# Two activation groups transposed per visit in the second feed-forward, and a ScalarE copy of the query projections ahead of their norm

## The chip, the cores and the metric

The kernel runs on one core of one Trainium2 chip. The metric is the device time of one execution in microseconds; before the change it is 2654.88 us, the median of three runs (2654.12 to 2655.74). The engines are named as the profile names them: PE is TensorE's matmul (PEld its weight load), ACT is ScalarE, DVE is VectorE, POOL is GpSimd, SP is SyncE.

## What is computed

One layer of a diffusion backbone over 256 latent tokens and 256 context tokens of width 2048, all in float32: a half-step SwiGLU feed-forward, a mixing sub-layer, and a second half-step SwiGLU on the latent tokens alone. The mixing sub-layer projects the tokens to the queries of 8 heads, keys and values of 2 heads, and the three inputs of a long convolution; a gate from one of the three is multiplied in at the end. The two places that the change touches are these:

```python
def q_heads(p_q, q_norm):
    B, L = p_q.shape[:2]
    return rms_norm(p_q.reshape(B, L, N_Q_HEADS, HEAD_DIM), q_norm)

def swiglu(h, w_up, w_down):
    gate, up = jnp.split(h @ w_up, 2, axis=-1)
    return (jax.nn.silu(gate) * up) @ w_down
```

Each head's 128 query values are divided by the root of their mean square, get a gain, are rotated (rope) and go into a softmax attention over 512 keys. The second feed-forward has 5632 hidden columns.

## The kernel before, in words

**Number format.** Every float32 operand of a large product is split into a high part (the float32 value rounded by an ACT cast) and a low part (the remainder, a DVE subtraction), and a product is three matmuls: high by high, high by low, low by high. For the weights `weight` does this (L207 to L229): a DMA of 512 KB into `raw` (four buffers), the cast L221 into `whi` (three buffers), the subtraction L225 into `wlo` (three buffers). For activations `split_to` does it (L201 cast, L202 subtraction).

**Buffers.** Most activation tiles come from one pool of 58 buffers of 2 KB per partition, tag `u` (function `U`). PSUM has two tags of four banks each: `pa` for the accumulations over the model width, `pb` for transposes, scores and the rest. The order of the instructions on each engine is worked out by a scheduler when the program is built: it starts from program order, and lets work that is ready go ahead of work that waits. So PE's order in the attention mixes several parts of the program.

**The queries.** Two groups of four heads (loop `qb`, L1068). For each group `proj_steps` (L822 to L834) accumulates two `pa` banks, one for each half of 128 tokens, over eight weight pieces (matmuls L831 to L833, 12 for a piece). The first group's projection is issued in steps among the long convolution's transforms (L232 to L234 at that place). Then `fill` issues the first half of the gate's first projection (`proj_pair`, matmuls L239, L240, L242, two more `pa` banks). `head_norm` (L865) takes one `pa` bank: Square on ACT (L869) out of PSUM, a sum over each head on DVE (L871), `rstd_from` (L262 to L271, with a Sqrt on ACT at L263), and a DVE multiply out of PSUM (L874) into a `u` tile. `gain_rope` (L877) asks for another `u` tile and applies gain and rotation in ten DVE operations (L882 to L899; its first result is L895). Four PE transposes (L1078) and a split follow, and `attend` runs scores, softmax (L1045 to L1051), transposes (L1058) and products for the two halves. The second query group's projection is the next user of `pa` after the gate's first one. `head_norm` is also called with two heads for the keys, four times.

**After the attention.** The rest of the gate (L240), the group norms (L1094 to L1102), and the output projection (`out_unit`, with `tok_mm`, L1118 to L1120), then the norm of the second feed-forward.

**The second feed-forward.** The up stage has 22 groups (`UPG`) of 256 hidden columns. A group has two `pa` banks (128 tokens each) and eight weight pieces of 12 matmuls (L1118 to L1120). At its end ACT makes Silu of the gate half (L1311), DVE multiplies the up half (L1312), and the result `at` holds 256 tokens by 256 columns with tokens on the partitions. The down stage needs it the other way round, so `turn_act` transposes it on PE into one `pb` bank (four transposes of 128x128, L1275) and splits that into two tiles (L201, L202). It is called for the group before, after the third weight piece of the current group (`kp == 2`); for the last group it is called in the down stage, at its third weight piece (`fq == 2`). The first 14 of the 44 split tiles have a pool of their own (`act`), the others are `u` tiles. The down stage has four column blocks of 22 weight pieces, again 12 matmuls for a piece.

Of the kernel before, what the change touches and what calls it, by code (L numbers as in the profile page):

```python
# [18 lines left out]
P = 128  # L19
D = 2048  # L20
KT = D // P
L = 256
# [33 lines left out]
def hybrid_layer_kernel(ctx: ExitStack, tc: tile.TileContext, a):  # L56
    nc = tc.nc
    V, S, G, PE = nc.vector, nc.scalar, nc.gpsimd, nc.tensor
    serial = [0]

    def T(pool, shape, tag, dt=F32, bufs=None):
        serial[0] += 1
        kw = {} if bufs is None else {"bufs": bufs}
        return pool.tile(list(shape), dt, tag=tag, name=f"{tag}_{serial[0]}", **kw)
# [6 lines left out]
    def U(shape, dt=F32):  # L71
        return T(up, shape, "u", dt, 58)

    def tmp(shape):
        return T(up, shape, "sq", bufs=2)

    def tmp2(shape):
        return T(up, shape, "sg", bufs=3)

    def PA(shape=(P, 512)):  # L80
        return T(pp, shape, "pa")

    def PB(shape=(P, 512)):
        return T(pp, shape, "pb")

    ident = T(const, (P, P), "ident")
# [91 lines left out]
    def ada_col(d):  # L178

        bank = ada_bank.pop(d)  # L180
        rows = tmp2((P, 2 * P))
        copied = S.copy(rows, bank[:, 0 : 2 * P])
        for j in range(2):
            last = PE.transpose(bank[:, (2 + j) * P : (3 + j) * P], rows[:, j * P : (j + 1) * P], ident)
        col = cols[d % 2]
        turned = bank[:, 2 * P : 4 * P].rearrange("p (j g c) -> p j c g", g=4, c=32)
        V.tensor_reduce(col, turned[:, :, 0:2, :], axis=AX.X, op=ALU.add)
        V.scalar_tensor_tensor(first_mod[:, 1, d, :], col[:, 0, :], bada1[:, d : d + 1],
                               gn[:, 0, d : d + 1].broadcast_to((P, 2)), op0=ALU.add, op1=ALU.mult)
        V.tensor_scalar(first_mod[:, 0, d, :], col[:, 1, :], bada[:, d : d + 1], None, op0=ALU.add)  # L190
        return copied, last, bank
# [8 lines left out]
    def split_to(src, hi, lo):  # L200
        S.copy(hi, src)  # L201
        V.tensor_sub(lo, src, hi.bitcast(F32))  # L202
        return hi, lo
# [55 lines left out]
    def rstd_from(ss, n, shape, pool_tile, y, root=None):  # L259

        m, e = pool_tile(shape), pool_tile(shape)
        mean = V.tensor_scalar(m, ss, 1.0 / n, EPS, op0=ALU.mult, op1=ALU.add)  # L262
        rooted = S.activation(y, m, AF.Sqrt)  # L263
        roots.append(rooted)
        if root:
            then(root(mean, rooted), V.reciprocal, y, y)
        else:
            V.reciprocal(y, y)
        V.tensor_mul(e, y, y)
        V.scalar_tensor_tensor(e, e, -0.5, m, op0=ALU.mult, op1=ALU.mult)  # L270
        return V.scalar_tensor_tensor(y, e, 1.5, y, op0=ALU.add, op1=ALU.mult)  # L271
# [277 lines left out]
    for i in range(2):  # L549
        for q in range(KT // 2):  # L550
            t = U((P, 2, L))
# [151 lines left out]
    with tc.issue_after(mm.ins), tc.issue_after(scaled.ins), tc.issue_after(shifted.ins):  # L703
        copied, mm, _ = ada_col(1)
# [130 lines left out]
    def small(shape):  # L835
        return T(mp, shape, "small", bufs=8)
# [28 lines left out]
    def head_norm(ps, nh):  # L865

        sq = tmp((P, nh, P))
        pv = ps[:, 0 : nh * P].rearrange("p (h d) -> p h d", d=P)
        S.activation(sq, pv, AF.Square)  # L869
        ss, r_ = small((P, nh)), small((P, nh))  # L870
        V.tensor_reduce(ss, sq, axis=AX.X, op=ALU.add)  # L871
        rstd_from(ss, P, (P, nh), small, r_)
        o = U((P, nh, P))
        V.tensor_mul(o, pv, r_.unsqueeze(2).broadcast_to((P, nh, P)))  # L874
        return o

# [48 lines left out]
    for kv in range(2):  # L925
        pt = PB()
# [51 lines left out]
    for half in range(2):  # L978
        hs = slice(half * 512, half * 512 + 512)
        vt = []  # L980
        for t in range(2):
            pt = PB((P, 4, P))
# [85 lines left out]
    for qb in range(2):  # L1068
# [4 lines left out]
        for t in range(2):  # L1073
            n_ = head_norm(pq[t], 4)
            r = gain_rope(n_, 4, 0, t)
            pt = PB()
# [37 lines left out]
    def tok_mm(ps, x, w, start, stop, ttiles=(0, 1)):  # L1114

        for t in ttiles:
            hi, lo = (x_[:, t * P : (t + 1) * P] for x_ in x)
            PE.matmul(ps[t], hi, w[0], start=start, stop=False)  # L1118
            PE.matmul(ps[t], hi, w[1], start=False, stop=False)  # L1119
            last = PE.matmul(ps[t], lo, w[0], start=False, stop=stop)  # L1120
        return last

    def out_unit(g, b, late=1):

        ps = [PA(), PA()]
        held = []
        for kp in range(4):
            held.append(weight(a["w_o"][b, 4 * g + kp], (P, 2, 512)))
            if 4 - late <= kp < 3:
                continue  # L1130
            for t in range(2):
                for n, (whi, wlo) in enumerate(held):
                    for k2 in range(2):
                        k = 2 * (kp + 1 - len(held) + n) + k2
                        last = tok_mm(ps, [y[8 * g + k][:, s, :] for s in range(2)], (whi[:, k2, :], wlo[:, k2, :]), k == 0, k == 7, (t,))
            held = []
        return ps, last
# [12 lines left out]
    for b in range(NB):  # L1150
        ps, _ = out_unit(0, b)
# [26 lines left out]
    def mod_x(d, src):  # L1178
        m_ = T(up, (P, L), "mt", bufs=3)[:, 0 : src.shape[1]]
        return m_, S.activation(m_, src, AF.Identity, bias=mod[0][6][:, d : d + 1], scale=mod[0][7][:, d : d + 1])  # L1180
# [9 lines left out]
    def scaled_x(t, b):  # L1190
        xn = U((P, 512))
        return xn, V.tensor_scalar(xn, xt[t][b], rs2[:, t : t + 1], None, op0=ALU.mult)

    def turned(xn):
        pt = PB((P, 4, P))
        for d in range(4):
            PE.transpose(pt[:, d, :], xn[:, d * P : (d + 1) * P], ident)
        return pt
# [26 lines left out]
    pt = turned(xn)  # L1225
    hh = [h[d][:, :, 0:P] for d in range(4)]
    added = then(scaled, out_add, ps, rh, NB - 1, 1)
    m_, _ = mod_x(0, pt[:, 0, :])
# [16 lines left out]
    xn, _ = scaled_x(1, 0)  # L1245
# [19 lines left out]
    acts = []  # L1265

    def act_tile(n):
        shape = (P, 2, L)
        return U(shape, F32R) if n >= EXTRA else T(fp, shape, "act", F32R, EXTRA)

    def turn_act(g, at):
        pt = PB((P, 2, L))
        for f in range(2):
            for t in range(2):
                PE.transpose(pt[:, f, t * P : (t + 1) * P], at[:, t, f * P : (f + 1) * P], ident)  # L1275
        acts.append(split_to(pt, act_tile(2 * g), act_tile(2 * g + 1)))

    prev = None
    for g in range(UPG):
        ps = [PA(), PA()]  # L1280
        behind = None
        if g == 0:
            for t in range(2):
                for k in range(4):
                    tok_mm(ps, [h[k][:, s, :] for s in range(2)], ws[k], k == 0, False, (t,))
                if t == 0:
                    pt = turned(xn)
                    for d in range(4):
                        hi, lo = mod2(d, pt[:, d, :], h[d][:, :, P:L])
                        behind = behind or (lo, hi)  # L1290
            rest_h(1)
        for kp in range(8):
            if g == 0 and kp < 2:
                continue
            if g == 0 and kp == 2:
                pieces = ws[4:6]
            else:
                late = dict(zip(("behind", "behind_hi"), behind)) if g == 0 and kp < 6 else {}
                whi, wlo = weight(a["w_up2"][g, kp], (P, 2, 512), **late)
                pieces = [(whi[:, k2, :], wlo[:, k2, :]) for k2 in range(2)]  # L1300
            for k2 in range(2):
                k = 2 * kp + k2
                tok_mm(ps, [h[k][:, s, :] for s in range(2)], pieces[k2], k == 0, k == KT - 1)
            if g == 0 and kp in (2, 4):
                rest_h(kp // 2 + 1)
            if kp == 2 and prev:
                turn_act(*prev)
        at = U((P, 2, L))
        for t in range(2):
            sg = tmp2((P, L))  # L1310
            S.activation(sg, ps[t][:, 0:L], AF.Silu)  # L1311
            V.tensor_mul(at[:, t, :], ps[t][:, L : 2 * L], sg)  # L1312
        prev = (g, at)
    h = None
    for b in range(NB):
        ps = [PA(), PA()]
        for fq in range(UPG):
            whi, wlo = weight(a["w_dn2"][b, fq], (P, 2, 512))
            if b == 0 and fq == UPG // 2:
                grow = gate_row(1)  # L1320
            if b == 0 and fq == 2:
                turn_act(*prev)
            for t, f in ((0, 0), (1, 0), (0, 1), (1, 1)) if fq < UPG - 1 else ((0, 0), (0, 1), (1, 0), (1, 1)):
                tok_mm(ps, [t_[:, f, :] for t_ in acts[fq]], (whi[:, f, :], wlo[:, f, :]), fq + f == 0, fq == UPG - 1 and f == 1, (t,))
        for t in range(2):
            o = tmp2((P, 512))
            V.tensor_mul(o, ps[t], grow[b])
            V.tensor_add(xt[t][b], xt[t][b], o)
            nc.sync.dma_start(a["out"][t, :, b * 512 : (b + 1) * 512], xt[t][b])
# [126 lines left out]
```

## Time and profile before

| | before |
|---|---|
| median of three runs | 2654.88 us (2654.12 to 2655.74) |
| the profiled execution | 2655.01 us |
| its span, first to last instruction | 2653.2 us |
| PE busy | 2632.3 us, 99% |
| DVE busy | 1723.7 us, 65% |
| ACT busy | 942.2 us, 36% |
| matmuls | 12482 |

A row of instructions in the profile gives line, engine, operation, what it writes and reads by the program's names (buffer numbers left out), the shapes and the count; idle time stands behind it, with what ended it. Matmuls overlap: one of 512 columns is shown with 0.39 us, though one starts every 0.23 us, so the distance between starts is what counts on PE. The first line of an instruction's group is its line in the kernel; a helper's line can serve many places.

### The profile page before, as it was taken

The page shows a single profiled execution, that of the slowest core. Times are in us where ns is not written, and L with a number is a line of the kernel's source. Part 1 is how long each engine was busy: PE and PEld are TensorE (multiplying, and loading weights), DVE is VectorE, ACT ScalarE, POOL GpSimd, SP SyncE. Part 2 cuts the span into 40 slices and gives each one's busy share as a digit, 9 for nine tenths or more (in the row PEclk, how much of TensorE's full clock was granted, in tenths as well). Part 3 has the DMA queues.
Part 4 walks back from the last instruction along what each step waited for, and adds up shares of the span by engine and source line. Part 5 has one row for each costly group of instructions (what it writes and reads, how often), then busy time and mean ns, then how long its engine had stood idle before and what let it go on. Part 6 is the DMA issues. An engine that isn't in the chain of part 4 may idle for free.

```text
span 2653.2 us, 32468 instructions
## 1 busy us (share of the span) xinstructions
PE 2632.3 (99%) x12482; PEld 2167.3 (82%) x12482; DVE 1723.7 (65%) x2707; ACT 942.2 (36%) x1242; POOL 21.2 (1%) x44
## 2 busy tenths in 40 slices
PE   8999999999999999999999999999999999999999
PEld 5678888888888888888888988888788888888887
DVE  6789899976696666533333696889665555554444
ACT  5333222222222222222222465456554444444333
POOL 1100000000000000000000000000000000000000
PEclk8999999999999999999999999999999999999999
DMA  9976656565686565632222455335555555556664
GB/s 364 364 247 213 217 209 235 207 233 211 229 286 244 203 228 213 212 98 101 95 96 95 134 173 195 126 129 164 169 184 189 191 190 191 189 188 206 202 201 157
DMA packets 143575, 515.78 MB, mean 194 GB/s; under 512 B 16699, under 2 KB 19708, under 8 KB 139068
## 3 DMA queue, kind: packets, MB, share of 16 engines
q1 hardware_dynamic: 140012, 501.77, 55.1%
q0 software_dynamic: 2784, 9.18, 1.0%
q10 hardware_dynamic: 624, 2.75, 0.3%
q8 instruction: 98, 1.61, 0.2%
q14 instruction: 57, 0.47, 0.0%
HBM read 509.43 MB, written 4.21 MB: 194 GB/s over the span
## 4 chain that ended last, share of the span: by engine, by line
PE 97%; DMA 1%; DVE 1%; ACT 0%; issue 0%; SPq 0%; DVEq 0%; ACTq 0%
PE pa L232 12%; PE pa L233 12%; PE pa L234 12%; PE pa L1119 10%; PE pa L1120 10%; PE pa L1118 10%; PE pb L232 7%; PE pb L233 7%; PE pb L234 7%; PE pa L240 3%; PE pa L242 2%; PE pb L175 1%; PE pa L832 1%; PE pa L833 1%; PE pa L831 1%; DMA wrow<-in_w_ada_dram 1%
## 5 line engine op out<-in xcount | busy, mean ns | idle before, releaser
L225 DVE TENSOR_TENSOR wlo<-raw,whi 128x1024 fp32r<-128x1024 f32 x639 | 781.2, 1223 | 634.3 <-ACT whi L221 623.1
L221 ACT CAST whi<-raw 128x1024 fp32r<-128x1024 f32 x639 | 672.2, 1052 | 1330.2 <-PE pa L233 473.7
L232 PE MATMUL pa<-u,whi 128*128 128x512 f32 x1376 | 538.3, 392 | 2.1 <-ACT u L644 2.1
L233 PE MATMUL pa<-u,whi 128*128 128x512 f32 x1376 | 536.2, 390 | 0.4 <-DVE u L649 0.4
L234 PE MATMUL pa<-u,wlo 128*128 128x512 f32 x1376 | 535.9, 390 | 0.0
L1118 PE MATMUL pa<-whi,u 128*128 128x512 f32 x1060 | 413.9, 391 | 0.0
L1119 PE MATMUL pa<-wlo,u 128*128 128x512 f32 x1060 | 412.8, 390 | 0.2 <-DVE wlo L225 0.2
L1120 PE MATMUL pa<-whi,u 128*128 128x512 f32 x1060 | 412.8, 390 | 0.0
L232 PEld LDWEIGHTS pa<-u,whi 128*128 128x128 f32 x1376 | 258.2, 188 | 61.6 <-issue 4.5
L233 PEld LDWEIGHTS pa<-u,whi 128*128 128x128 f32 x1376 | 258.5, 188 | 54.3 <-DVE u L649 1.5
L234 PEld LDWEIGHTS pa<-u,wlo 128*128 128x128 f32 x1376 | 258.5, 188 | 53.9
L232 PE MATMUL pb<-u,whi 128*128 128x512 f32 (+1 forms) x800 | 299.5, 375 | 0.0
L233 PE MATMUL pb<-u,whi 128*128 128x512 f32 (+1 forms) x800 | 297.8, 372 | 0.0
L234 PE MATMUL pb<-u,wlo 128*128 128x512 f32 (+1 forms) x800 | 297.7, 372 | 0.0
L1119 PEld LDWEIGHTS pa<-wlo,u 128*128 128x128 f32 x1060 | 199.1, 188 | 41.4 <-DVE wlo L225 0.6
L1120 PEld LDWEIGHTS pa<-whi,u 128*128 128x128 f32 x1060 | 199.0, 188 | 41.3
L1118 PEld LDWEIGHTS pa<-whi,u 128*128 128x128 f32 x1060 | 199.0, 188 | 40.7
L138 DVE CUSTOM_DVE_ANT_0 adas<-adaw,crow,mod 128x1024 bf16<-128x1024 f32 x160 | 205.2, 1282 | 28.4 <-DMA adaw<-in_w_adaT_dram 25.7
L138 DVE CUSTOM_DVE_ANT_0 adas<-adaw,crow,cond 128x1024 bf16<-128x1024 f32 x160 | 204.9, 1280 | 20.4 <-DMA adaw<-in_w_adaT_dram 18.6
L232 PEld LDWEIGHTS pb<-u,whi 128*128 128x128 f32 x800 | 150.6, 188 | 28.2 <-issue 2.1
L233 PEld LDWEIGHTS pb<-u,whi 128*128 128x128 f32 x800 | 150.7, 188 | 26.4 <-issue 0.4
L234 PEld LDWEIGHTS pb<-u,wlo 128*128 128x128 f32 x800 | 150.7, 188 | 26.3
(290 smaller groups left out, 2131.4 us busy)
## 6 DMA issues: line engine op xcount, KB each, us to landing
raw<-in_w_up_dram SPq DMA_DIRECT2D x340, 512.0 KB, 3.3
adaw<-in_w_adaT_dram SPq DMA_DIRECT2D x223, 512.0 KB, 5.0
raw<-in_w_dn_dram SPq DMA_DIRECT2D x184, 512.0 KB, 4.1
wrow<-in_w_ada_dram SPq DMA_DIRECT2D x32, 1024.0 KB, 9.4
raw<-in_w_hy_dram SPq DMA_DIRECT2D x32, 512.0 KB, 3.3
raw<-in_w_o_dram SPq DMA_DIRECT2D x32, 512.0 KB, 3.4
raw<-in_w_kv_dram SPq DMA_DIRECT2D x16, 512.0 KB, 3.6
raw<-in_w_q_dram SPq DMA_DIRECT2D x16, 512.0 KB, 3.3
```

The source lines that it names most:

```text
L138: V.tensor_tensor_reduce(out=sc, in0=t, in1=crow[i][:, b * (D // 2) : (b + 1) * (D // 2)], scale=1.0, scalar=mcol if b else bada[:, n : n ...
L175: last = PE.matmul(bank[g : g + 32, 0 : 2 * P], cs[:, k, :], t[:, k8, :], start=k < 4, stop=k >= KT - 4)
L221: S.copy(hi, raw)
L225: V.tensor_sub(lo, raw, hi.bitcast(F32))
L232: PE.matmul(ps, w[0], xx[0], start=start, stop=False)
L233: PE.matmul(ps, w[0], xx[1], start=False, stop=False)
L234: return PE.matmul(ps, w[1], xx[0], start=False, stop=stop)
L240: PE.matmul(ps, w[0], x, start=start, stop=stop)
L242: PE.matmul(ps[:, 0, :], w[1], x[:, 0, :], start=False, stop=False)
L1118: PE.matmul(ps[t], hi, w[0], start=start, stop=False)
L1119: PE.matmul(ps[t], hi, w[1], start=False, stop=False)
L1120: last = PE.matmul(ps[t], lo, w[0], start=False, stop=stop)
```

## The change

`head_norm` gets a copy for the calls with four heads, which are the queries: ACT copies the PSUM bank into the result tile `o`, the Square reads that copy, and the multiply works in place on it. For the keys (two heads) nothing changes but the place where `o` is asked for. In the second feed-forward `turn_acts` takes a list of groups: the results of two groups are kept, and after the third weight piece of every other group both are transposed one after the other into two `pb` banks and then split. Groups 20 and 21 are transposed in the down stage, at the place where before group 21 alone was.

```diff
@@ head_norm
         sq = tmp((P, nh, P))
         pv = ps[:, 0 : nh * P].rearrange("p (h d) -> p h d", d=P)
+        o = U((P, nh, P))
+        if nh == 4:
+
+            S.copy(o, pv)
+            pv = o
         S.activation(sq, pv, AF.Square)
         ss, r_ = small((P, nh)), small((P, nh))
         V.tensor_reduce(ss, sq, axis=AX.X, op=ALU.add)
         rstd_from(ss, P, (P, nh), small, r_)
-        o = U((P, nh, P))
         V.tensor_mul(o, pv, r_.unsqueeze(2).broadcast_to((P, nh, P)))
         return o
@@ second feed-forward
-    def turn_act(g, at):
-        pt = PB((P, 2, L))
-        for f in range(2):
-            for t in range(2):
-                PE.transpose(pt[:, f, t * P : (t + 1) * P], at[:, t, f * P : (f + 1) * P], ident)
-        acts.append(split_to(pt, act_tile(2 * g), act_tile(2 * g + 1)))
-
-    prev = None
+    def turn_acts(pairs):
+
+        pts = []
+        for _, at in pairs:
+            pts.append(PB((P, 2, L)))
+            for f in range(2):
+                for t in range(2):
+                    PE.transpose(pts[-1][:, f, t * P : (t + 1) * P], at[:, t, f * P : (f + 1) * P], ident)
+        for (g, _), pt in zip(pairs, pts):
+            acts.append(split_to(pt, act_tile(2 * g), act_tile(2 * g + 1)))
+
+    prev = []
@@ up stage
-            if kp == 2 and prev:
-                turn_act(*prev)
+            if kp == 2 and len(prev) == 2:
+                turn_acts(prev)
+                prev = []
...
-        prev = (g, at)
+        prev.append((g, at))
@@ down stage
             if b == 0 and fq == 2:
-                turn_act(*prev)
+                turn_acts(prev)
```

## Rows read from the trace of the kernel before

**Rows 1.** The page: busy time of each engine, and the clock row.
```profile
PE 2632.3 (99%) x12482; PEld 2167.3 (82%) x12482; DVE 1723.7 (65%) x2707; ACT 942.2 (36%) x1242; POOL 21.2 (1%) x44
...
PEclk8999999999999999999999999999999999999999
```

**Rows 2.** What PE waited for from 1700 us on: total, times, longest (us).
```profile
PE pa L831 <- DVE small L269: 1.2, 1, 1.2
PE pa L1118 <- ACT u L1229: 0.9, 1, 0.9
```

**Rows 3.** Timeline of PE: start, length (us), instruction, idle before and its end.
```profile
1728.35 0.47 PE L831 MATMUL pa<-whi,u 128*128 128x512 f32 x1 [1.17 <-DVE small L269]
```

**Rows 4.** Timeline of ACT at the first query group's norm.
```profile
1715.15 0.60 ACT L869 ACTIVATE sq<-pa 128x512 f32<-128x512 f32 x1 [0.24 <-PE pa L833]
...
1716.65 1.05 ACT L221 CAST whi<-raw 128x1024 fp32r<-128x1024 f32 x1
```

**Rows 5.** Timeline of DVE at the end of the same norm.
```profile
1725.62 1.19 DVE L225 TENSOR_TENSOR wlo<-raw,whi 128x1024 fp32r<-128x1024 f32 x1
...
1727.52 0.68 DVE L874 TENSOR_TENSOR u<-pa,small 128x512 f32<-128x512 f32 x1
...
1730.37 0.42 DVE L895 TENSOR_TENSOR u<-sg,sg 128x256 f32<-128x256 f32 x1
```

**Rows 6.** Groups by line and shape from 1540 us: busy us, mean ns, idle.
```profile
L1275 PE MATMUL pb<-ident,u 128*128 128x128 f32 x88 | 13.2, 272 | 0.0
...
L1328 DVE TENSOR_TENSOR u<-u,sg 128x512 f32<-128x512 f32 x8 | 5.2, 684 | 0.1
...
L846 ACT COPY u<-pb 128x512 f32<-128x512 f32 x8 | 4.6, 575 | 0.0
...
L1098 ACT ACTIVATE sq<-u 128x512 f32<-128x512 f32 x6 | 3.8, 626 | 0.0
...
L874 DVE TENSOR_TENSOR u<-pa,small 128x512 f32<-128x512 f32 x4 | 2.7, 686 | 0.1
```

**Rows 7.** Windows: length; PE, PEld, DVE, ACT, POOL busy; clock, DMA share, GB/s.
```profile
14.00:28.00 14.00, 10.38 (x61) 5.87 (x60) 9.07 (x26) 6.19 (x13) 0.00 (x0) 0.63 1.00 397
...
1770.00:1785.00 15.00, 15.00 (x90) 13.12 (x89) 14.60 (x34) 8.23 (x12) 0.00 (x0) 1.00 0.53 174
2420.00:2640.00 220.00, 220.00 (x972) 182.16 (x971) 106.15 (x93) 85.46 (x81) 0.00 (x0) 1.00 0.61 199
```

**Rows 8.** Timelines of ACT and DVE at the second query group's norm.
```profile
1768.92 1.06 ACT L221 CAST whi<-raw 128x1024 fp32r<-128x1024 f32 x1
...
1770.01 1.23 DVE L225 TENSOR_TENSOR wlo<-raw,whi 128x1024 fp32r<-128x1024 f32 x1
...
1778.07 0.42 DVE L895 TENSOR_TENSOR u<-sg,sg 128x256 f32<-128x256 f32 x1
```

**Rows 9.** The chain that ended last, in order of time: start, length (us), what.
```profile
1675.04 0.87 PE pb L985 x8
...
1772.38 0.46 PE pa L240 x2
...
1949.59 0.44 PE pb L1275 x4
...
2394.52 0.44 PE pb L1275 x4
```

**Rows 10.** Timeline of PE at the first transposes of the second feed-forward.
```profile
1949.42 0.60 PE L1275 MATMUL pb<-ident,u 128*128 128x128 f32 x4
```

**Rows 11.** Timelines of ACT and DVE behind these transposes.
```profile
1950.58 0.58 ACT L201 CAST act<-pb 128x512 fp32r<-128x512 f32 x1
1952.83 1.05 ACT L221 CAST whi<-raw 128x1024 fp32r<-128x1024 f32 x1 [1.67 <-PE pa L1120]
...
1951.85 0.68 DVE L202 TENSOR_TENSOR act<-pb,act 128x512 fp32r<-128x512 f32 x1
1953.91 1.23 DVE L225 TENSOR_TENSOR wlo<-raw,whi 128x1024 fp32r<-128x1024 f32 x1 [1.38 <-ACT whi L221]
```

## Prediction

> **What bounds the kernel now.** I read the page first [rows 1]: TensorE (PE) is busy 99% of the span, 2632.3 of 2653.2 us, ScalarE (ACT) 36%, VectorE (DVE) 65%; the clock row stands at full speed in all slices but the first. So the whole program has 20.9 us in which PE does nothing, and an edit that takes no PE work away can win only from these. Next I asked what PE waits for from 1700 us on, because the first edit sits at 1715 us and the second from 1949 us. The longest wait there is one of 1.2 us, at line L831, the next one 0.9 us at L1118 [rows 2]. The change touches the first of these and nothing of the second, which lies in the norm ahead of the second feed-forward.
>
> The wait at L831 is the one place where the norm over heads stops PE [rows 3]. L831 is the first matmul of the second query projection, and the queries of the first one still hold its PSUM bank. The tag "pa" has four banks: two hold the first query projection, two the gate's. A bank of the queries comes free when its last reader has read it, and in the kernel before that is the multiply L874, not the Square. The Squares ran at 1715.15 [rows 4], but the multiply of the first half ran on DVE from 1727.52 for 0.68 us, behind a weight remainder (L225) and what else was queued there [rows 5]. PE went on at 1728.35, after 1.17 us idle, just after that multiply's end at 1728.20. The trace names a small operation beside it on DVE as releaser; the bank is the only thing that L831 lacks at that moment.
>
> **Part 1, the copy out of PSUM.** It applies to the calls with four heads: two halves of two query groups, four calls. Each adds one ACT copy of 128x512 from PSUM: 575 ns by the same operation at L846 [rows 6], so 4 x 0.575 = 2.3 us of ACT, which is idle 64% of the span. The Square is moved behind the copy and reads SBUF: 626 ns (L1098) for the 0.60 us that it takes from PSUM [rows 4, 6]. The multiply stays 686 ns: with both inputs in SBUF a DVE tensor by tensor operation of this size takes 684 (L1328) [rows 6]. So DVE's load is unchanged, and each norm's chain is longer by some 0.6 us. [...]
>
> What the copy removes is the wait. The Square had run at 1715.15, so a copy in its place frees the bank by about 1716, and even one that is held up by 6 us is early enough. Then PE can go on at 1727.1 with the second projection. Its weights allow that: the high part of the first piece was cast at 1716.65 [rows 4], and the remainder of the second was ready at 1726.8 (1725.62 + 1.19) [rows 5]. Gain at this place: 1.17 us.
>
> A bound on it: the output tile of the second half is asked for after the rope output of the first half, from the same pool. If buffers are handed out in program order, the second copy can't run before L895 at 1730.37 [rows 5]; its bank is then free at 1730.9. PE has the first half's matmuls of three weight pieces to run by then, 18 at 0.23 us (worked out below) or 4.1 us from 1727.1 to 1731.2. So the stall goes in either case.
>
> What is late next is DVE, which supplies the weight remainders. It is busy 14.60 of 15 us from 1770 to 1785 [rows 7]; a remainder that begins at 1770.01 and takes 1.23 us ends at 1771.24 [rows 8], for a piece that PE starts at 1772.38 [rows 9]: 1.14 us of slack, about what PE would be earlier. Its cast on ACT, at 1768.92, stands behind the second group's norm [rows 8], which now holds one or two copies more. So some of the 1.17 us may be lost there. Bounds: 0 to 1.2 us kept; I take 1.0, since ACT and DVE before this place wait for PE and are early too when PE is.
>
> **Part 2, transposes of two groups together.** The transposes are the same 88; the visits to them fall from 22 to 11. Price of a visit: from one visit to the next are (2394.52 - 1949.59)/20 = 22.247 us [rows 9]. The 96 matmuls of a group, at 220/971 = 0.2266 us each (972 touch that window, so 971 starts) [rows 7], take 21.75. A visit thus costs 0.49 us. Of it the bare transposes need 0.44: the four of a visit span 0.60 us [rows 10], the last one's own length is 0.27 (272 ns at L1275 [rows 6]), so three steps take 0.33 and one 0.11. Only some 0.05 us belongs to going there and back. Halving the visits saves at most 11 x 0.05 = 0.6 us. From below, if more than half of the extra goes with each bank that is read out and not with the visit, 11 x 0.02 = 0.2; a loss would need a wait. I take 0.4.
>
> A wait is unlikely. Once in two groups ACT gets one 0.58 us cast more in a row and DVE one 0.68 us remainder more [rows 11], and one in the next group less. Behind the casts ACT is idle 1.67 us until the next weight, DVE 1.38 us [rows 11]; both fit. The two transposed tiles need two of the four "pb" banks, which nothing else uses in this stage. The two last groups are turned early in the down stage (third of 22 weight pieces); their tiles are wanted only at pieces 20 and 21.
>
> **Sum.** The profiled execution took 2655.01 us (span 2653.2), 0.13 above the median of 2654.88. 1.0 + 0.4 = 1.4 off it gives 2653.6, and off the median 2653.5.
>
> **Rivals.** *The gain is given back* where DVE and ACT bind, at 1772 us or at the start of the output projection: part 1 is worth 0 to 0.3, part 2 0.2 to 0.4, time 2654.4. For it speak DVE's 14.60 of 15 us and the 1.14 us of slack; against it that ACT and DVE had waited for PE before.
>
> *The copy holds up ACT's queue, slower.* ACT works in order. In the second group the copy of the second half may have to wait for a buffer that goes first to the rope of the first half (L895 at 1778.07 [rows 8]). If it is queued ahead of the weight cast that ran at 1768.92, that cast waits with it. PE would come 1.0 us early, which leaves 0.14 of the 1.14 us of slack; every microsecond by which the cast is later than that is one that PE stands still, and the gains of 1.0 and 0.4 are spent when the cast is 1.5 us late: from that point it is slower. In the mild form (two copies and two Squares in front, 2 x 0.58 + 2 x 0.63 = 2.4 us) PE loses 2.3: 2654.9 - 1.4 + 2.3 = 2655.8. In the full form the cast waits from 1768.92 to 1778.07, 9.2 us, and PE loses 9.0: 2662.5. Against it: the casts on ACT are ordered around such waits all through this stage.
>
> *The clock falls.* Eight transposes in a row are 0.9 us without a matmul. The chain of waits has eight of them in a row at 1675.04 [rows 9], and the clock row keeps its full mark there [rows 1]; so from this trace nothing should happen. [...]
>
> *Nothing changes*: the two sets of transposes are issued apart as before, and the wait at L831 is then held by something else that ends at 1728: 2654.9.
>
> **How the numbers follow.** Forecast 2653.5: 0.55. Given back: 0.20. Slower by the queue: 0.13, of which the full form 0.04. No change: 0.11. Clock: 0.01. The range goes from the upper bounds of both parts (2654.9 - 1.2 - 0.6 = 2653.1) less 1.0 for another order around the attention, whose transposes share PE with the second projection (20 visits fewer at 0.05 us each), to the mild form of the queue with some of the same against it (8 visits more): 2652.1 to 2656.2; each end goes 0.5 further for the spread of the runs (2654.12 to 2655.74), to 2651.6 and 2656.7. About 0.2% (5.3 us) is what a measurement of this kernel can tell from no change. A gain of that size is not to be had from waits of 1.2 and 0.9 us, so faster 0.02; slower 0.05, the full form of the queue and the clock; same 0.93.
>
> **What would show it.** Right: no idle time at the first L831 of the second projection, copies on ACT at 1716 to 1722 ahead of the Squares, L1275 in runs of eight with 11 visits 44.5 us minus some 0.05 us apart, and the same clock. Wrong: a new wait of PE for L225 between 1770 and 1830 us, casts of L221 behind a copy that waits, or the wait at L831 still there.

## The result, and the profile after

| | before | after |
|---|---|---|
| median | 2654.86 us (22 runs) | 2658.53 us (22 runs) |
| ratio of the times, 95% interval | | 1.0015 (1.0009 to 1.0021) |
| span of the profiled execution | 2653.2 us | 2656.4 us |

The change makes the kernel slower by 0.15%, some 3.7 us. That is inside the 0.2% that I had called no change, but the interval excludes 1, the forecast had the other sign (2653.5), and the time lies outside the range (2651.6 to 2656.7).

The page of the changed kernel, busy time and clock, for [rows 1]:

```profile
PE 2634.9 (99%) x12482; PEld 2168.7 (82%) x12482; DVE 1726.1 (65%) x2707; ACT 945.0 (36%) x1246; POOL 21.2 (1%) x44
...
PEclk8999999999999999999999999999999999999999
```

Four more ACT instructions are there, the four copies. The number of matmuls and the clock row are unchanged. So the loss is time in which PE waits or switches between kinds of work (PE's busy time is 2.6 us longer for the same matmuls: where a start comes too late, the profile shows a part of the delay as busy, 0.28 of 0.82 us at 1780.12). What PE waited for from 1700 us on (total, times, longest in us), for [rows 2]:

```profile
PE pb L1082 <- DVE u L903: 1.1, 1, 1.1
PE pb L232 <- DVE u L197: 0.9, 1, 0.9
PE pa L1122 <- ACT u L1233: 0.9, 1, 0.9
PE pa L240 <- ACT whi L221: 0.6, 1, 0.6
PE pa L1122 <- ACT u L1192: 0.6, 2, 0.3
PE pa L242 <- DVE wlo L225: 0.5, 1, 0.5
PE pa L1123 <- DVE wlo L225: 0.5, 2, 0.3
PE pa L1122 <- ACT u L255: 0.2, 1, 0.2
```

The wait at L831 is gone. In its place PE waits 1.1 us for the rope's result (L903, L899 before the change) at the transposes of the first half's queries, then for weights at L240 and L242, then for a split at L232.

I cut both traces at two instructions that each has: the last transpose of the inputs ahead of the long convolution (L844), and the first matmul on `spin` (L1217, now L1221) in the norm ahead of the second feed-forward. Between them lie transforms, attention and output projection, the **attention stretch**; from there to PE's last instruction is the **feed-forward stretch**.

| | before | after | difference |
|---|---|---|---|
| attention stretch, us | 236.35 | 241.09 | +4.74 |
| feed-forward stretch, us | 736.94 | 736.07 | -0.87 |

The remaining -0.7 us lies ahead of both, where the program is the same; that part takes 1672.8 to 1675.8 us in all the traces here but one, so -0.7 is within what differs from trace to trace. So the pairs gained 0.87 us, and the copy lost 4.7.

Where the copies ran, ACT's timeline (start, length in us, instruction, idle before), for [rows 4]; the row ahead of each pair shows what they followed:

```profile
1719.59 1.13 ACT L196 CAST u<-u 128x512 fp32r<-128x512 f32 x2
1720.63 0.58 ACT L872 COPY u<-pa 128x512 f32<-128x512 f32 x1
1721.24 0.63 ACT L874 ACTIVATE sq<-u 128x512 f32<-128x512 f32 x1
...
1727.70 0.57 ACT L872 COPY u<-pa 128x512 f32<-128x512 f32 x1
...
1766.54 2.06 ACT L196 CAST u<-pb 128x512 fp32r<-128x512 f32 x4 [0.23 <-PE pb L1062]
1768.46 0.63 ACT L872 COPY u<-pa 128x512 f32<-128x512 f32 x1
...
1778.45 0.58 ACT L872 COPY u<-pa 128x512 f32<-128x512 f32 x1
```

The first Square ran at 1715.15 before [rows 4]; now copy and Square come 5 to 6 us later, right behind the last casts (L196) of the convolution's splits. In the second group the copy stands right behind the last casts of the attention's splits. The multiplies on DVE, whose rows before are at 1727.52, 1731.62, 1768.39 and 1781.49 (the first of them in [rows 5]), are these now, between three more rows of DVE that are used further down:

```profile
1729.66 0.69 DVE L878 TENSOR_TENSOR u<-u,small 128x512 f32<-128x512 f32 x1
...
1731.40 0.42 DVE L899 TENSOR_TENSOR u<-sg,sg 128x256 f32<-128x256 f32 x1
...
1737.58 0.68 DVE L878 TENSOR_TENSOR u<-u,small 128x512 f32<-128x512 f32 x1
...
1766.34 1.22 DVE L225 TENSOR_TENSOR wlo<-raw,whi 128x1024 fp32r<-128x1024 f32 x1 [0.25 <-ACT whi L221]
...
1776.57 0.69 DVE L878 TENSOR_TENSOR u<-u,small 128x512 f32<-128x512 f32 x1
...
1778.85 1.22 DVE L225 TENSOR_TENSOR wlo<-raw,whi 128x1024 fp32r<-128x1024 f32 x1
...
1786.17 0.68 DVE L878 TENSOR_TENSOR u<-u,small 128x512 f32<-128x512 f32 x1
```

The multiplies are later by 2.1, 6.0, 8.2 and 4.7 us. PE fills the time with the second query projection, which can start without the wait and has nothing to hold it: its last matmul (L833) starts at 1755.42, in the kernel before at 1766.13. At 1777 us PE has no such work left, and it stands at the gate's weights. PE's timeline there (idle before, and its end, in brackets), beside [rows 9]:

```profile
1778.60 0.99 PE L240 MATMUL pa<-u,whi 128*128 128x512 f32 x2 [0.56 <-ACT whi L221]
1780.12 0.51 PE L242 MATMUL pa<-u,wlo 128*128 128x256 f32 x2 [0.54 <-DVE wlo L225]
```

The L242 there starts right after the remainder that began at 1778.85. DVE had made none since 1766.34 (the kernel before has four in that time, at 1770.01, 1771.24, 1774.01 and 1778.48), and just ahead of it ran the second group's late multiply (1776.57) and the first steps of its rope. From 1770 to 1780 the weight stream stands almost still. Windows of the changed kernel (us, busy time of PE, PEld, DVE, ACT and POOL with counts, granted clock, DMA share, GB/s), the longer one for [rows 7]:

```profile
1770.00:1785.00 15.00, 13.91 (x75) 11.17 (x74) 12.38 (x35) 10.11 (x17) 0.00 (x0) 1.00 0.16 50
1770.00:1780.00 10.00, 9.03 (x45) 6.83 (x43) 7.38 (x21) 8.04 (x14) 0.00 (x0) 1.00 0.02 7
```

Between starts of PE instructions, steps that are over 0.15 us too long add up to 1.64 us before and 5.17 us after, from the last input transpose to the first matmul of the output projection; the small steps (switches between kinds of work) to 2.93 and 3.52 us. Together +4.1 us; the rest of the 4.7 comes in the output projection (a step of 0.45 us too much at 1831.85 among it).

### The profile page after: what moved, and what is told of

It reads as the page before. It is cut to its first block, busy times and chain, and to the rows that moved or that the text cites. A ratio compares the mean times of both kernels' runs of the same rounds, so it can differ in the third digit from the quotient of the medians.

```text
span 2656.4 us, 32469 instructions
## 1 busy us (share of the span) xinstructions
PE 2634.9 (99%) x12482; PEld 2168.7 (82%) x12482; DVE 1726.1 (65%) x2707; ACT 945.0 (36%) x1246; POOL 21.2 (1%) x44
## 4 chain that ended last, share of the span: by engine, by line
PE 96%; DVE 2%; DMA 1%; ACT 1%; issue 0%; SPq 0%; ACTq 0%; DVEq 0%
PE pa L232 12%; PE pa L233 12%; PE pa L234 12%; PE pa L1123 10%; PE pa L1124 10%; PE pa L1122 10%; PE pb L232 7%; PE pb L233 7%; PE pb L234 7%; PE pa L240 3%; PE pa L242 2%; PE pb L175 1%; PE pa L832 1%; PE pa L833 1%; PE pa L831 1%; DMA wrow<-in_w_ada_dram 1%
## 5 line engine op out<-in xcount | busy, mean ns | idle before, releaser
L232 PE MATMUL pa<-u,whi 128*128 128x512 f32 x1376 | 538.3, 392 | 2.1 <-ACT u L644 2.1
L232 PEld LDWEIGHTS pa<-u,whi 128*128 128x128 f32 x1376 | 258.2, 188 | 61.6 <-issue 4.5
L232 PE MATMUL pb<-u,whi 128*128 128x512 f32 (+1 forms) x800 | 299.5, 375 | 0.0
L232 PEld LDWEIGHTS pb<-u,whi 128*128 128x128 f32 x800 | 150.6, 188 | 28.2 <-issue 2.0
```

What stands on the lines that cost most here:

```text
L232: PE.matmul(ps, w[0], xx[0], start=start, stop=False)
```

## The experiments

My theory after reading the two traces: the copy needs a tile of the tag `u` as its output, such tiles go out in the order of the program, and with the copy ahead of it the whole norm now stands in that line. Before, only the multiply did; Square, sum and factor went ahead. Rivals: the 0.6 us by which each chain is longer; the pairs; too few buffers; and, between the two query groups, which of them makes the loss.

The difference in the table is median minus the median of the kernel before, measured beside it. "Waits" is the sum of the profile's waits of PE from 1700 to 1860 us, 1.2 us in the kernel before.

| kernel | median, us | difference | ratio, 95% interval | attention stretch | feed-forward stretch | waits |
|---|---|---|---|---|---|---|
| changed kernel | 2658.53 | +3.7 | 1.0009 to 1.0021 | 241.09 | 736.07 | 3.4 |
| 1 copy only | 2659.57 | +4.8 | 1.0010 to 1.0028 | 241.19 | 736.96 | 3.4 |
| 2 pairs only | 2653.91 | -0.8 | 0.9989 to 1.0007 | 236.41 | 736.10 | 1.2 |
| 3 copy, own buffers | 2653.62 | -1.1 | 0.9985 to 1.0003 | 235.52 | 736.96 | 0 |
| 4 Square twice | 2655.90 | +1.2 | 0.9995 to 1.0013 | 238.04 | 736.94 | 1.9 |
| 5 own buffers, 56 of `u` | 2653.70 | -1.2 | 0.9987 to 1.0005 | 235.30 | 736.99 | 0 |
| 6 own buffers and pairs | 2653.43 | -1.4 | 0.9986 to 1.0004 | 235.48 | 736.07 | 0 |
| 7 Square first, copy into `u` | 2654.51 | -0.4 | 0.9989 to 1.0007 | 236.05 | 736.98 | 0 |
| 8 copy, first group only | 2656.14 | +1.3 | 0.9995 to 1.0013 | 237.59 | 737.00 | 1.8 |
| 9 early first write | 2660.94 | +6.0 | 1.0011 to 1.0028 | 241.42 | 736.97 | 4.0 |
| 10 early request | 2659.31 | +4.4 | 1.0008 to 1.0025 | 241.29 | 736.96 | 3.4 |
| 11 own buffers, fours | 2652.48 | -2.5 | 0.9982 to 1.0000 | 235.50 | 735.96 | 0 |
| 12 own, Square first, pairs | 2654.26 | -0.7 | 0.9992 to 1.0009 | 237.17 | 736.10 | 1.1 |
| 13 first group only, early | 2655.13 | +0.3 | 0.9990 to 1.0008 | 236.20 | 736.98 | 0.4 |
| 14 both, first early | 2655.06 | +0.2 | 0.9991 to 1.0009 | 236.52 | 736.94 | 0.6 |
| 15 both, second early | 2655.00 | +0.2 | 0.9992 to 1.0010 | 236.17 | 736.94 | 1.1 |

An interval is about 0.09% to each side (2.4 us), so of the differences of kernels 1 to 15 only those of 1, 9 and 10 stand clear of zero by their times. For the others the stretches of the traces carry the reading: the feed-forward stretch, which most of the edits don't touch, lies within 0.06 us in all kernels without pairs, the kernel before among them (736.94 to 737.00), and within 0.03 us in the four with pairs (736.07 to 736.10). The attention stretch repeats as well where kernels should be alike: 236.35 and 236.41 (the kernel before, 2), 241.09, 241.19 and 241.29 (the changed kernel, 1, 10), 235.48 to 235.52 (3, 6, 11). The profiled execution of kernel 1 was a long one, 2667.04 us, and what it has too much lies ahead of both stretches (1682.0 us).

**Kernels 1 and 2: each part alone.**

```diff
 kernel 1: head_norm of the change, turn_act as before
 kernel 2: turn_acts of the change, head_norm as before
```

> The copy ahead of the norm alone; the second feed-forward turns its groups one by one as before. Theory (buffer order): the whole loss comes from the copy, because Square, sum and multiply of the queries now all stand behind a buffer of the tag u, which is handed out in program order; the stretch from the first pass over the queries' weights to the output projection is 4.1 us longer, and the time is that of the changed kernel plus the 0.87 us that its second feed-forward gained, about 2659.4 (+4.5 on the kernel before). Rival (the pairs share in the loss, through the order of work that the planner makes of the whole program): clearly less, +1 to +3.5. In both, no wait at the first matmul of the second query projection.

> The pairs of the second feed-forward alone; the norm over heads as before. Theory: a gain of 0.87 us in the second feed-forward and nothing else, 2654.0 (-0.9). My prediction's term for this part was 0.4, with 0.2 to 0.6 as bounds. Rival (the 0.87 us came from something that the copy moved, as where the norm ahead of that stage begins): 0.4 or less, 2654.5.

The loss is the copy's alone: its attention stretch is that of the changed kernel, with the same waits. The pairs gain 0.84 us in their stretch and touch nothing else.

**Kernel 3: the same copies, into buffers of their own.**

```diff
-        o = U((P, nh, P))
+        o = T(mp, (P, nh, P), "qn", bufs=2) if nh == 4 else U((P, nh, P))
         if nh == 4:
             S.copy(o, pv)
             pv = o
```

> The copy stays, ahead of the Square, but it goes into two buffers of its own instead of one of the tag u; groups turned one by one. Theory (buffer order): the copies run where the Squares ran before, some 5 to 12 us earlier than in the changed kernel; the wait of 1.2 us at the second projection is gone and the waits behind the norm are not there or are under 0.5 us each, so the time is 2653.7 to 2655 (-1.2 to 0). Rival (the copy's own 0.6 us in each chain, and its load on ScalarE): the loss stays, 2658 to 2659.5 (+3 to +4.5).

ACT's timeline of kernel 3:

```profile
1714.10 0.59 ACT L871 COPY qn<-pa 128x512 f32<-128x512 f32 x1 [0.25 <-PE pa L833]
1715.10 0.64 ACT L873 ACTIVATE sq<-qn 128x512 f32<-128x512 f32 x1
...
1759.76 0.57 ACT L871 COPY qn<-pa 128x512 f32<-128x512 f32 x1
```

Now the first copy starts when PE has finished the projection, and PE's waits between 1700 and 1860 us are all gone, the old one and the new ones. The copy, its 0.6 us in the chain and its 2.3 us of ACT are as in the changed kernel. What differs is when it may begin.

**Kernel 4: a longer chain without a copy.** The Square of the queries is done twice; only work is repeated.

```diff
+        if nh == 4:
+            S.activation(sq, pv, AF.Square)
         S.activation(sq, pv, AF.Square)
```

> No copy: the kernel before with the Square of the queries done twice, so that each of the four chains is longer by 0.6 us on ScalarE and the rest stands as before. The result is the same; only work is repeated. Theory (buffer order): the Squares ran 10 us ahead of the multiply, so 0.6 us more in front of it costs nothing or almost nothing, 2654.9 to 2655.4 (0 to +0.5). Rival (length of the chain): +2 to +4.5.

The expectation of 0 to 0.5 was too low: the stretch is 1.69 us longer. The old wait at L831 stays, and this one is added:

```profile
PE pa L242 <- DVE wlo L225: 0.7, 1, 0.7
```

So 0.6 us of chain isn't free here. It can't be the main cause, as kernel 3 has it too and its stretch is 0.83 us shorter than in the kernel before. It is a first sign of how little slack the weight remainders have near 1780 us, where DVE is busy 14.60 of 15 us [rows 7].

**Kernels 5 and 6: the same memory; and both parts.** Kernel 5 is kernel 3 with 56 buffers of `u`; kernel 6 is kernel 3 with the pairs.

```diff
-        return T(up, shape, "u", dt, 58)
+        return T(up, shape, "u", dt, 56)
```

> As the kernel with two buffers of its own for the copies, but the tag u has 56 buffers instead of 58: no more memory than the changed kernel has. It tells whether the place in the line for a u buffer costs the time or the lack of buffers. Theory (order of the line): the copies still run when the projection is ready, at about 1714 to 1717 and 1760 to 1765 us, and the time stays below that of the kernel before, 2653.6 (-1.1, at most 0). Rival (too few buffers in all): the copies or what follows them wait again and a loss of +2 to +4.5 returns, 2657 to 2659.

> The changed kernel with its copies put into two buffers of their own: both parts, without the wait for a u buffer. Theory: the two gains add, -1.1 from the copy (as the copy with its own buffers gave alone) and -0.8 to -0.9 from the pairs, 2652.9 (-1.9), which is ahead of both kernels. Rival (the gains overlap, or the planner's order of the whole program changes with the pairs): -1.0 or less, 2653.7 or more.

Two buffers fewer change nothing, so it isn't a lack of buffers. In kernel 6 the two gains add up in the stretches (-0.87 and -0.87), but the median is 1.4 us lower, between the 1.9 expected and the rival's 1.0, and its interval includes no change. A larger `u` wasn't tried.

**Kernel 7: only copy and multiply behind the line.**

```diff
         sq = tmp((P, nh, P))
         pv = ps[:, 0 : nh * P].rearrange("p (h d) -> p h d", d=P)
+        S.activation(sq, pv, AF.Square)
         o = U((P, nh, P))
         if nh == 4:
             S.copy(o, pv)
             pv = o
-        S.activation(sq, pv, AF.Square)
```

> The copy alone, again into a u buffer, but the Square goes first and reads PSUM as in the kernel before; groups turned one by one. So sum and factor of the norm run ahead of the buffer, and only copy and multiply stand behind it. Theory (the loss is that the statistics of the norm stand behind the buffer): Squares at about 1715 us, copies still at 1720 to 1728, and most of the 4.5 us gone: 2655 to 2656 (0 to +1.3). Rival (the loss is that the copy itself comes late and holds bank, ScalarE and multiply): 2658 to 2659.5 (+3 to +4.5).

ACT's timeline of kernel 7, first Square and first copy:

```profile
1716.12 0.60 ACT L869 ACTIVATE sq<-pa 128x512 f32<-128x512 f32 x1 [0.24 <-PE pa L833]
...
1725.97 0.57 ACT L872 COPY u<-pa 128x512 f32<-128x512 f32 x1
```

The four copies ran from 1726.0 to 1776.3, late as in the changed kernel (the first 5 us later still, the last 2 us earlier), the Squares from 1716.1 to 1764.1; PE has none of the waits, and the stretch is 0.30 us shorter than before the change. So here a late copy alone does no harm, and with the statistics behind it, as in kernel 1, the stretch is 5.1 us longer. Kernel 7 takes one change of order for this, and no memory.

**Kernel 8: the first group only.** `head_norm` copies for `qb == 0` only.

> The copy alone, into a u buffer ahead of the Square, for the first query group only; the second group has its norm as before. It tells in which group the loss arises. In the changed kernel the wait behind the first group (at the transposes of its queries, 1.1 us) is as long as the one that went (1.2), and the waits on weights at 1777 to 1780 (1.8 us) and at 1820 (1.05) stand behind the second. Theory (each group loses by its own late norm): +0.5 to +1.5, 2655.2 to 2656.2. Rival (the late start of the first group makes all of the later waits): +3 to +4.5, 2658 to 2659.5.

```profile
PE pb L1081 <- DVE u L902: 1.1, 1, 1.1
PE pb L232 <- DVE u L197: 0.7, 1, 0.7
```

The first group's lateness alone makes the wait at the queries' transposes and, later, one at a split, +1.24 us in the stretch; the waits on weights aren't there.

**Kernels 9 and 10: what gets a place in the line.** Both have the copies of the changed kernel, into `u`, from 58 buffers. The tiles are asked for earlier; in kernel 9 each also has a first write there.

```diff
     pq0 = []
+    slots = [U((P, 4, P)) for _ in range(2)]
+    for s_ in slots:                              # kernel 9 only
+        V.memset(s_[:, 0, 0:1], 0.0)              # kernel 9 only
...
+        if qb == 0:
+            slots = ...                           # the same, for the second group
         attend(qb)
```

> The copy alone, ahead of the Square and into a u buffer as in the changed kernel, 58 buffers. But the four result tiles get a first write earlier in the program: one column is set to zero by VectorE, for the first group ahead of the projection, for the second ahead of the first attention. Each holds its buffer longer for it. Theory (a u buffer goes out with the first write, and first writes are served in program order): the copies run when the projection is ready, at 1714 to 1717 and 1760 to 1765 us, and the time is that of the copies in buffers of their own, 2653.7 (-1.1). Rival (the copies wait because too few u buffers are there): holding four of them longer makes it no better, 2658 or more.

> The same without the four small writes: the result tiles are only asked for at the earlier place, and the copy is their first write. Theory (it is the first write that has a place in the line, not the request): copies where the changed kernel has them, behind the last casts of the transforms (1720 to 1728 us) and of the attention (1768 to 1778), and its loss, 2659.4 (+4.5). Rival (the request has the place): 2653.7 (-1.1).

Kernel 10 is the changed kernel again, copies and waits alike. ACT's first copy in kernel 10, then two of kernel 9:

```profile
1720.70 0.58 ACT L872 COPY u<-pa 128x512 f32<-128x512 f32 x1
```

```profile
1714.53 0.59 ACT L872 COPY u<-pa 128x512 f32<-128x512 f32 x1 [0.30 <-PE pa L833]
...
1760.10 0.59 ACT L872 COPY u<-pa 128x512 f32<-128x512 f32 x1 [1.04 <-PE pa L833]
```

With a first write early in the program the same copies into the same pool run as soon as the projection ends. So it is the place of the first write in the program that decides when a tile is had, not the request and not the number of buffers. But kernel 9 lost 6.0 us, by other waits and a lower clock behind one of them; this part of the expectation was wrong. PE's waits in kernel 9, then its timeline there, then the remainder's start on DVE, then the windows:

```profile
PE pa L242 <- DVE wlo L225: 2.4, 1, 2.4
PE pb L1120 <- DVE u L1113: 1.2, 1, 1.2
```

```profile
1780.60 0.79 PE L242 MATMUL pa<-u,wlo 128*128 128x256 f32 x2 [2.43 <-DVE wlo L225]
1781.19 0.63 PE L240 MATMUL pa<-u,whi 128*128 128x512 f32 x1
1781.61 0.41 PE L242 MATMUL pa<-u,wlo 128*128 128x256 f32 x1
```

```profile
1776.09 1.05 ACT L221 CAST whi<-raw 128x1024 fp32r<-128x1024 f32 x1 [1.57 <-PE pa L240]
...
1779.32 1.22 DVE L225 TENSOR_TENSOR wlo<-raw,whi 128x1024 fp32r<-128x1024 f32 x1
```

```profile
1776.00:1780.00 4.00, 1.72 (x10) 0.88 (x8) 4.00 (x12) 1.63 (x2) 0.00 (x0) 1.00 0.00 0
1780.00:1784.00 4.00, 3.40 (x12) 2.95 (x13) 3.48 (x5) 0.00 (x0) 0.00 (x0) 0.57 0.49 153
```

The piece was cast by 1777.14, but its remainder began only at 1779.32: in DVE's queue it stood behind the rope of both halves, and DVE was busy without a gap from 1776 to 1780. Behind the wait the granted clock is low (0.57): four pairs of a 512- and a 256-column matmul start 0.64 us apart (from 1781.19), where such pairs had been 0.35 apart (up to 1775.65). By these rows I estimate 1.1 us of the loss for it.

**Kernels 13 to 15: which early write does that.** Kernel 13: copy and early write for the first group alone. Kernel 14: both copies, early write for the first group. Kernel 15: both copies, early write for the second.

> The copy for the first query group only, into u buffers that get their small first write early; the second group has its norm as before the change. To be held beside the copy for the first group without the early write (+1.3). Theory (a late norm costs the time, and an early first write mends it): copies at 1714 to 1717, no wait at the second projection nor at the transposes of the first group's queries, and -0.5 to -1.2, 2653.8 to 2654.4. Rival (the early first write, by the buffers that it holds, does the harm that the version with four of them showed): +1 or more.

> Both groups' copies into u buffers, the early first write for the first group alone. Theory (each group pays for its own late norm): the wait at the first group's transposes gone, those on weights at 1777 to 1780 us and at 1820 there, +2 to +4. Rival (the waits from 1777 us on come from the first group): -0.5 to -1.2.

> Both groups' copies into u buffers, the early first write for the second group alone. With the version that had both written early (+6.0, second group's copies early and yet waits of 2.4 and 1.2 us for weight remainders): if the second group's early write is what harms, through the order in which VectorE takes remainders and rope, the wait for a remainder near 1778 us is here too, and the loss is +4 to +7. If the two early writes harm only together, the wait near 1778 us is under 1 us and the loss is that of the first group, +1 to +2.

PE's waits from 1700 to 1860 us in kernels 13, 14 and 15, one each:

```profile
PE pa L242 <- DVE wlo L225: 0.4, 1, 0.4
```

```profile
PE pa L240 <- ACT whi L221: 0.6, 1, 0.6
```

```profile
PE pb L1083 <- DVE u L903: 1.1, 1, 1.1
```

Neither early write does harm alone. In kernel 13 the waits of kernel 8 are gone, though its time, +0.3, and its stretch, -0.15, fall short of the gain that was expected. Kernels 14 and 15 each mend one group and bring back nearly all of the loss (stretch +0.17 and -0.18): with the first group early the wait at its transposes goes, and of those on weights 0.6 us stay; with the second early all of those go. So the expectation that each group pays for itself was wrong. With the first group alone late the stretch is +1.24 (kernel 8) or -0.18 (kernel 15), with the second alone +0.17 (kernel 14), with both +4.8. My reading is that one late norm finds other work for PE, and after the first there is none left for the second; no run tests that by itself.

**Kernels 11 and 12: looking for a better version.**

```diff
 kernel 11, on kernel 6
-            if kp == 2 and len(prev) == 2:
+            if kp == 2 and len(prev) == 4:
 kernel 12, on kernel 6: the Square stands ahead of the copy and reads PSUM
```

> Copies in two buffers of their own, and the second feed-forward turns four groups together instead of two: 6 visits instead of 11 (22 before), sixteen transposes in a row. From the pairs, a visit that falls away is worth 0.87/11 = 0.08 us. Theory (the price goes with the visit): 5 visits fewer are 0.4 us, the up stage from the first to the last visit shows it, and the time is 2653.0. Rival (four banks and four casts in a row make TensorE wait, or its clock fall): +0.5 or more on the version with pairs, or a granted clock under 1.00 in that stage.

> Copies in two buffers of their own and pairs, with the Square first, out of PSUM: the statistics of the norm no longer stand behind the copy, the bank is given back 0.6 us later. Theory (the length of a chain that is not held up matters little): as the version with the copy first, 2653.4, within 0.4. Rival (0.6 us of chain is worth a microsecond, as the Square done twice may mean): 2652.5 or less.

Kernel 11 has the lowest median, 2652.48, but its span is that of kernel 6 (2650.6 both), and its feed-forward stretch is only 0.11 us shorter where 0.4 was expected; that it is faster than kernel 6 isn't shown. Kernel 12 has 1.1 us of waits on weights, at L240 and L242, which kernel 6 hasn't; the shorter chain gained nothing, and its stretch is 1.7 us longer than that of kernel 6. Like kernel 4 it has no norm that waits for a `u` tile ahead of its Square: 0.6 us of repeated work (kernel 4) or a change of order (kernel 12) can each move the stretch by 1.7 us, and single differences of that size, such as the +1.24 of kernel 8, are no safe price of one step.

## Why the prediction was wrong, point by point

**What bounds the kernel: right.** The loss is waits and switches of PE; its work is the same.

**The wait at L831: right.** It goes in every kernel with a copy of the first group, and PE goes on at once. The copy came at 1720.63 instead of 1716, and that was early enough for the bank, as the text said.

**"Each norm's chain is longer by some 0.6 us": this is the step that failed.** I gave the copy the place of the Square, 1715.15, and added 0.6. But the tile `o` moved up with it, from the multiply to the copy, and with it everything that reads the copy. I had even written that the second copy can't run before the first rope if buffers go out in program order, and used that for the bank and, in a rival, for a weight cast on ACT; I didn't follow Square, sum, factor, multiply, rope and transposes behind it. Nor did I ask what else stands in that line: the convolution's and the attention's splits, which come first in the program. Measured: multiplies later by 2.1 to 8.2 us, transposes of the second half's queries at 1742.73 instead of 1737.14, and 4.7 us more in the attention stretch. Kernels 3 and 7 take this away and keep the copy. The bound itself was wrong as I put it: the second copy ran at 1727.70, ahead of the rope's first result (L899, 1731.40). As I read it, the order by first writes is one in which tiles are planned, not one in which the writes must run.

**"What is late next is DVE", 0 to 1.2 us: the place was right, the size and the sign were not.** PE did come to stand at weights near 1778 us, which was one of my signs of being wrong. My bound assumed that part 1 can lose no more than it gains. The runs show no such end: kernel 9 has 2.4 us at one remainder.

**The multiply at 684 ns from either memory: right**, 0.68 to 0.69 us from SBUF, against 686 ns from PSUM [rows 6].

**Part 2, 0.4 us with 0.2 to 0.6: the right sign, mis-sized.** The pairs gained 0.84 to 0.87 us in the four traces that have them. Visits in the changed kernel, PE's timeline, for [rows 9, 10]:

```profile
1975.24 1.03 PE L1282 MATMUL pb<-ident,u 128*128 128x128 f32 x8
...
2019.66 1.03 PE L1282 MATMUL pb<-ident,u 128*128 128x128 f32 x8
...
2374.96 1.03 PE L1282 MATMUL pb<-ident,u 128*128 128x128 f32 x8
```

Two groups take (2374.96 - 1975.24)/9 = 44.413 us, against 2 x 22.247 = 44.494: 0.081 a visit, where I had 0.05. Of this the transposes and the switch give 0.01 (four transposes and both switches cost 0.446 us over plain matmuls, eight cost 0.882). The other 0.07 lies in the matmuls after a visit: in the kernel before, of the nine that follow a visit all but one start 229 to 236 ns apart instead of 227; after a visit of eight transposes only two are that long. Kernel 11 shows that this isn't a price for each visit: four groups take 88.807 us there, 0.02 less than with pairs. What lengthens those matmuls in the kernel before stays open.

**Rivals.** *Given back* (2654.4) named the place, not the size. *The copy holds up ACT's queue*, 2655.8 to 2662.5: the time lies between, but by another mechanism; ACT did cast no weight from 1766.3 to 1774.89, but no copy waited at the head of its queue in that time (none has idle time in front of it); the copies were queued late. That ACT works in order is seen in the kernel before: it stood idle for 6.55 us until a copy (L182) could run at 32.02 us, and a weight cast (L567) whose data had landed at 28.13 ran behind that copy, at 32.29. *Nothing changes*: no, the wait at L831 went and the transposes stand in runs of eight. *The clock*: [rows 1] and the page after agree; sixteen transposes in a row leave it at 1.00 as well, as this window of kernel 11 shows, with a visit at 2101.89:

```profile
2101.00:2105.00 4.00, 4.00 (x27) 3.56 (x26) 2.51 (x4) 2.70 (x5) 0.00 (x0) 1.00 0.56 190
```

From 1949 to 2414 us, over the visits of the up stage, the granted clock is 1.00 in the changed kernel (eight in a row) and in kernel 11 (sixteen); no run here gives this rival a size.

**The range** left out the case that decided, a norm that stands as a whole behind another line. And 0.2% was too coarse a bound: 22 runs tell 0.06%.

What is shown: the loss is in the attention stretch and comes from the copy (1, 2); the place of the copy's first write in the program sets when the copy runs (9 against 10), and the loss goes when the copies have buffers of their own (3, 5), when one group's first write is early (14, 15) or when the statistics stay ahead of the copy (7); with only one group late the full loss isn't there (8, 14, 15), with both late it is (1, 10). But kernel 9 loses as much with the copies of both groups early, so early copies aren't enough. What isn't shown: why kernel 9 gets a worse order on DVE than kernel 5, whose copies are as early. It was not settled whether the buffers held or the small writes move the scheduler's order.

## What to carry to other kernels

When an edit moves the first write of a pooled tile ahead of other steps, as here, all these steps move into that pool's line; ask what stands in that line ahead of them and follow the whole chain to the next work of the bound engine, not just the one wait that the edit removes. A staging copy wants buffers of its own, or only the step that must free the bank behind it: where it shares a pool, statistics that can read the source directly should stay ahead of the copy (with buffers of its own that order gained nothing, kernel 12). Where the bound engine fills its waits with other work, a wait that goes may only spend that work earlier, and the next wait finds none; that is how I read the second group here.

## What the hardware showed beyond that

PE's clock fell after one long wait. In kernel 9 PE was busy 1.72 of 4 us up to 1780 (waits of 0.44 and 2.43 us), and the granted clock of the next 4 us is 0.57: there its matmuls of 512 and 256 columns take 0.63 and 0.41 us, instead of 0.40 (from 1783.74 on) and 0.28 (at 1775.89). Single waits of 1.1 to 1.2 us, in the kernel before at 1727 and in the changed one at 1731 us, left it at 1.00 (windows from 1722 to 1732 and from 1731 to 1735 us).
